# SwiGLU on one core: one activation and one product for each two-row tile in place of one for each row

**The chip and the metric.** The kernel runs on one core of one Trainium2 chip. The metric is the device time of one execution in microseconds (us). Three runs of the kernel before gave 936.18 us in the median (936.04 to 936.34).

## The reference

```python
# x: 8192 x 8192, float32, normal random numbers
def reference(x):
    a, b = np.split(x, 2, axis=-1)
    silu_b = b / (1 + np.exp(-b))
    return a * silu_b                 # 8192 x 4096
```

Each input row holds 4096 values `a` and then 4096 gates `b`. The kernel must read 268.44 MB and write 134.22 MB. It does two operations of arithmetic on each output: a silu and a product.

## The kernel before

A tile holds 128 partitions with two rows each, so a partition holds `a0 b0 a1 b1`, 4096 floats each: 64 KB. There are 32 tiles and three buffers. ScalarE (ACT) overwrites `b` with silu(b), and VectorE (DVE) writes the product over `a`. Row 1's product goes over `b0`, which row 0's product has read by then, so that both results lie side by side and leave in one store. SyncE (SP) issues the loads. ACT issues the stores, apart from the last three, which SP issues.

```python
    R, BUFS = 2, 3
    # ... last = 31
    def swiglu(i, k, c0=0, cw=half):
        xt = tiles[i]
        b = xt[:, k * M + half + c0 : k * M + half + c0 + cw]
        nc.scalar.activation(out=b, in_=b, func=_SILU)
        nc.vector.tensor_mul(
            out=xt[:, k * half + c0 : k * half + c0 + cw],
            in0=xt[:, k * M + c0 : k * M + c0 + cw],
            in1=b,
        )
    # ...
    for i in range(BUFS):
        load(i)
    for i in range(last):
        for k in range(R):
            swiglu(i, k)
        if i == last - 1:
            swiglu(last, 0)
        store(i)
        nxt = i + BUFS
        if nxt < last:
            load(nxt)              # waits until store(i) has landed
        elif nxt == last:
            load(last, (0, 1))     # the last tile comes in two halves
            load(last, (1, 2))
    store(last, 0, half)
    # ... the last row in two pieces, then its store
```

Of the kernel before, what the change touches and what calls it, by code (L numbers as in the profile page):

```python
# [1 line left out]

# [4 lines left out]

_SILU = mybir.ActivationFunctionType.Silu


@with_exitstack
def kernel(
    ctx: ExitStack,
    tc: tile.TileContext,
    x: bass.AP,
    out: bass.AP,
):




    nc = tc.nc
    N, M = x.shape
    half = M // 2
    P = nc.NUM_PARTITIONS
    R = 2
    BUFS = 3

    xv = x.tensor.reshape([N // R, R * M]).ap()  # L30
    ov = out.tensor.reshape([N // R, R * half]).ap()
    ntiles = N // (P * R)
    last = ntiles - 1

    pool = ctx.enter_context(tc.tile_pool(name="sbuf", bufs=BUFS))
    ctx.enter_context(tc.manual_schedule())
    tiles = {}

    def load(i, rows=None):
        if i not in tiles:  # L40
            tiles[i] = pool.tile([P, R * M], x.dtype, name="xt")
        lo, hi = (0, R) if rows is None else rows
        nc.sync.dma_start(  # L43
            out=tiles[i][:, lo * M : hi * M], in_=xv[i * P : (i + 1) * P, lo * M : hi * M]
# [9 lines that stand above are left out]
            in1=b,  # L54
        )

    def store(i, c0=0, cw=R * half):
        (nc.scalar if i < last - 1 else nc.sync).dma_start(
            out=ov[i * P : (i + 1) * P, c0 : c0 + cw], in_=tiles[i][:, c0 : c0 + cw]
        )  # L60

    for i in range(BUFS):
        load(i)
    for i in range(last):
        for k in range(R):
            swiglu(i, k)
        if i == last - 1:
            swiglu(last, 0)
        store(i)
        nxt = i + BUFS  # L70
        if nxt < last:
            load(nxt)
        elif nxt == last:
            load(last, (0, 1))
            load(last, (1, 2))

    store(last, 0, half)
    for c0 in range(0, half, half // 2):
        swiglu(last, 1, c0, half // 2)
    store(last, half, half)  # L80


# [1 line left out]
_INS = ['x']  # L84
_OUTS = [((8192, 4096), 'float32')]


# [23 lines left out]
```

## Time and profile before

| | before |
|---|---|
| span of the profiled run | 934.8 us |
| DVE / ACT busy | 30% / 25% |
| DMA rate in the steady part | 434 GB/s, share 1.00 |
| round of one buffer | 87.0 us: load 34.4, compute 12.6, store 39.7 |
| period of a tile | 29.0 us |

What a load or a store takes beyond the 29.0 us of a tile is waiting behind another one in its queue: 5.4 us for the load and 10.6 for the store that the prediction follows. "Queueing" below means this waiting, and "room" means the queueing of a load and a store together; the prediction works both out.

### The profile page before, as it was taken

Reading aid. Unit: us, or ns where it says so; the run is one execution under the profiler, and the core shown is the slowest. Engines: PE = TensorE matmul, PEld = TensorE weight load, DVE = VectorE, ACT = ScalarE, POOL = GpSimd, SP = SyncE. Lnnn points to the kernel's source line nnn. Section 1 sums busy time; section 2 is a strip of 40 time slices with the busy share of each in tenths; the row PEclk is TensorE's granted clock in tenths of the full one; section 3 lists DMA queues with packets and bytes.
Section 4 is the critical chain, followed back from the end, with each engine's and each line's share of the span. In section 5 each row is a group of like instructions: output and inputs, shape, how many; then the busy total and the mean of one; then the engine's idle time right before and its main releaser. Section 6 shows DMA issues by size and latency. Waiting matters only on the chain.

```text
span 934.8 us, 367 instructions
## 1 busy us (share of the span) xinstructions
DVE 283.3 (30%) x65; ACT 229.4 (25%) x66; POOL 0.2 (0%) x4
## 2 busy tenths in 40 slices
DVE  0333312333123331133321333213332133331242
ACT  0223320233302333113331133311333203332041
POOL 0000000000000000000000000000000000000000
DMA  9999999999999999999999999999999999999998
GB/s 404 400 445 430 430 439 433 428 435 443 428 430 439 429 442 432 435 426 453 419 430 452 411 452 423 428 447 425 433 433 453 414 443 429 426 447 428 425 437 376
DMA packets 9506, 402.67 MB, mean 431 GB/s; under 512 B 1056, under 2 KB 1056, under 8 KB 1056
## 3 DMA queue, kind: packets, MB, share of 16 engines
q1 hardware_dynamic: 5184, 276.83, 68.6%
q10 hardware_dynamic: 4320, 125.83, 31.2%
q14 instruction: 2, 0.02, 0.0%
HBM read 268.44 MB, written 134.22 MB: 431 GB/s over the span
## 4 chain that ended last, share of the span: by engine, by line
DMA 84%; DVE 10%; ACT 4%; DVEq 0%; issue 0%; SPq 0%; ACTq 0%
DMA out_dram<-xt 42%; DMA xt<-in_x_dram 42%; DVE xt L51 10%; ACT xt L50 4%; DVEq L106 0%; SPq L43 0%; ACTq L50 0%; DVEq L51 0%
## 5 line engine op out<-in xcount | busy, mean ns | idle before, releaser
L51 DVE TENSOR_TENSOR xt<-xt 128x4096 f32<-128x4096 f32 (+1 forms) x65 | 283.3, 4359 | 637.7 <-ACT xt L50 634.5
L50 ACT ACTIVATE xt<-xt 128x4096 f32<-128x4096 f32 (+1 forms) x65 | 228.1, 3556 | 688.1 <-DMA xt<-in_x_dram 688.1
L50 ACT ACT_TABLE_LOAD x1 | 1.3, 1283 | 0.7 <-PEq L95 0.7
L95 POOL MEMSET const-bfloat16-1.0<- 128x1 bf16 x1 | 0.1, 103 | 0.0
L95 POOL MEMSET const-uint8-127<- 128x1 uint8 x1 | 0.1, 102 | 0.0
L95 POOL MEMSET const-float32-0.0<- 128x1 f32 x1 | 0.1, 100 | 0.2 <-issue 0.2
L95 POOL MEMSET const-float32-1.0<- 128x1 f32 x1 | 0.1, 99 | 0.0
## 6 DMA issues: line engine op xcount, KB each, us to landing
out_dram<-xt ACTq DMA_DIRECT2D x30, 4096.0 KB, 39.7
xt<-in_x_dram SPq DMA_DIRECT2D x2, 4096.0 KB, 27.1
out_dram<-xt SPq DMA_DIRECT2D x1, 4096.0 KB, 23.6
out_dram<-xt SPq DMA_DIRECT2D x2, 2048.0 KB, 14.5
xt<-in_x_dram SPq DMA_DIRECT2D x31, 34.5
```

The source lines that it names most:

```text
L50: nc.scalar.activation(out=b, in_=b, func=_SILU)
L51: nc.vector.tensor_mul(out=xt[:, k * half + c0 : k * half + c0 + cw], in0=xt[:, k * M + c0 : k * M + c0 + cw], in1=b,)
L95: nc = _bacc.Bacc("TRN2", target_bir_lowering=False, num_devices=1)
```

## The change

The intent is fewer and longer instructions: one activation over both gates of a tile and one product over both rows, in place of two each. The product reads `a0 a1` against `b0 b1` and writes its 8192 results to the front of the tile. The second half of its output therefore lies over `b0`, an input of the same instruction. The last tile keeps its pieces.

```diff
+    def swiglu_tile(i):
+        rows = tiles[i].rearrange("p (k s c) -> p k s c", k=R, s=2)
+        b = rows[:, :, 1, :]
+        nc.scalar.activation(out=b, in_=b, func=_SILU)
+        nc.vector.tensor_mul(
+            out=tiles[i][:, : R * half].rearrange("p (k c) -> p k c", k=R),
+            in0=rows[:, :, 0, :],
+            in1=b,
+        )
@@
     for i in range(last):
-        for k in range(R):
-            swiglu(i, k)
+        swiglu_tile(i)
```

## The prediction

Four passages that no trace of this case shows are cut from the prediction, and the cuts are marked. The first two, around the count of packets, set the rate, the sharing of the engines and the durations beside figures from elsewhere, and argued that the overlapping product would give right results at the rate of the product by rows. The third gave a reason for the small gain of rival 3, the fourth the reason for the 1% of rival 4. Rival 3's tenths and rival 4's 1% stand as guesses. No term of the sum is cut: it comes to 0 us, with 0 to 1 us for the load margin, so 936.4 against 936.18.

Two things that the prediction uses have their numbers in the packet records of the kernel before. A load's row (64 KB) took 2.418 us and a store's (32 KB) 1.213 in the median, and of those begun between 133 and 850 us 3167 were loads' and 3166 stores': 289 and 145 GB/s, two thirds and a third. And a transfer's start: load 0, issued at 0.73 us, had its first packet at 1.73. The "up to 2 us" of a restart in the range was a guess; no trace had shown a restart then, and the experiments below measured from nothing to about 1.8 us.

> **What bounds the kernel now.** I read first the page of the profile (busy shares, the span in slices), then the busy time by stage, then the chain that ended last, then the timeline of two tiles, and last the groups by shape. From the page:
>
> ```profile
> DVE 283.3 (30%) x65; ACT 229.4 (25%) x66; POOL 0.2 (0%) x4
> ...
> DMA  9999999999999999999999999999999999999998
> ...
> HBM read 268.44 MB, written 134.22 MB: 431 GB/s over the span
> ```
>
> The compute engines are busy 30% and 25% of the span; the DMA engines are at 90% or more in all slices but the last. The kernel does nothing but stream 402.67 MB through one core, so the first suspicion is that the stream sets the time. The stages say how close to its ceiling it is (columns: stretch, its length, busy time of DVE, ACT and POOL, clock, DMA share, GB/s):
>
> ```profile
> 22.00:35.00 13.00, 8.64 (x2) 7.12 (x2) 0.00 (x0) 1.00 1.00 434
> ...
> 46.00:75.00 29.00, 8.85 (x2) 7.12 (x2) 0.00 (x0) 1.00 1.00 434
> ...
> 400.00:429.00 29.00, 8.83 (x3) 7.10 (x3) 0.00 (x0) 1.00 1.00 434
> ```
>
> The share is 1.00 and the rate 434 GB/s, at 22 to 35 us (loads alone; no store is issued before 35.24 us) as in the middle (loads and stores together). At 434 GB/s the 402.67 MB take 927.8 us of a span of 934.8; the other 7 us are mostly start and end (nothing moves in the first microsecond, and the last 2.8 us move at 29 GB/s). So in the steady part there is almost no idle time of the DMA that a change of the computing could win back.
>
> The page's chain of work seems to object: it gives 84% to DMA, 10% to DVE and 4% to ACT, as though 14% were computing on the path. The chain in order of time shows one round of a buffer (columns: start, length, what; in us):
>
> ```profile
> 98.96 34.44 DMA xt<-in_x_dram
> ...
> 133.51 3.63 ACT xt L50
> ...
> 137.16 4.43 DVE xt L51
> ...
> 141.68 4.44 DVE xt L51
> ...
> 146.14 39.70 DMA out_dram<-xt
> ```
>
> A buffer goes round in load 34.44, compute 12.6 (133.51 to 146.12), store 39.70, and a few tenths of issue: 87.0 us. There are three buffers, so a tile passes every 29.0 us. Now 29.0 us is also what the bytes of one tile need: 8.39 MB in and 4.19 MB out, 12.58 MB / 434 GB/s = 29.0 us. Both descriptions give the same period, so one of them is slack. The timeline decides which (columns: start, length, engine and line, operation, count, idle time before it):
>
> ```profile
> 75.42 7.12 ACT L50 ACTIVATE xt<-xt 128x4096 f32<-128x4096 f32 x2 [21.87 <-DMA xt<-in_x_dram]
> 79.07 8.96 DVE L51 TENSOR_TENSOR xt<-xt 128x4096 f32<-128x4096 f32 x2 [20.04 <-ACT xt L50]
> 88.06 0.34 ACTq L58 DMA_DIRECT2D out_dram<-xt  x1
> 104.51 7.12 ACT L50 ACTIVATE xt<-xt 128x4096 f32<-128x4096 f32 x2 [21.96 <-DMA xt<-in_x_dram]
> 108.16 8.96 DVE L51 TENSOR_TENSOR xt<-xt 128x4096 f32<-128x4096 f32 x2 [20.13 <-ACT xt L50]
> 117.15 0.34 ACTq L58 DMA_DIRECT2D out_dram<-xt  x1
> ```
>
> The load issued at 98.96 lands at 133.40, but the load before it lands only at about 104.4 (ACT starts on it at 104.51): for 5.4 us of its 34.4 it waits behind another load. The store issued at 117.15 follows one issued at 88.06, which takes 39.7 and lands at about 127.8: it waits some 10.6 us behind a store. In the steady part there are thus always a load and a store under way, and the round carries 5.4 + 10.6 = 16.0 us of queueing. The DMA stream is the bound; compute counts on the chain only because it takes the place of queueing.
>
> [...] The page's count agrees with one packet per row: 4320 packets for 30 stores are 144 each, about 128 rows of 32 KB plus 16. A load's row is 64 KB, so a load gets about two thirds of the rate and a store a third, and both finish in about 29 us of service. [...]
>
> **The change part by part.** The durations come from the groups by shape:
>
> ```profile
> L51 DVE TENSOR_TENSOR xt<-xt 128x4096 f32<-128x4096 f32 x63 | 278.8, 4425 | 634.2 <-ACT xt L50 631.0
> L50 ACT ACTIVATE xt<-xt 128x4096 f32<-128x4096 f32 x63 | 224.4, 3608 | 682.1 <-DMA xt<-in_x_dram 682.1
> L51 DVE TENSOR_TENSOR xt<-xt 128x2048 f32<-128x2048 f32 x2 | 4.5, 2288 | 3.5 <-ACT xt L50 3.5
> L50 ACT ACTIVATE xt<-xt 128x2048 f32<-128x2048 f32 x2 | 3.7, 1901 | 6.0 <-DMA xt<-in_x_dram 6.0
> ```
>
> Slopes and fixed parts: DVE (4425-2288)/2048 = 1.043 ns an element and 151 ns fixed; ACT (3608-1901)/2048 = 0.833 and 194. The whole-tile forms have 8192 elements: DVE 151 + 8192 x 1.043 = 8.70 us, ACT 194 + 8192 x 0.833 = 7.02 us.
> - Removed on 31 tiles (tile 31 keeps its pieces): one ACTIVATE and one product each, so 62 instructions, and their fixed parts. DVE saves 2 x 4.425 - 8.70 = 0.15 us a tile, 4.7 us in all; ACT saves little, since neighbours overlap already (two take 7.12, one is to take 7.02), 0.1 a tile. Neither is on the path that sets the end: both engines idle about 20 us before each tile.
> - Moved: the first product used to begin after the first ACTIVATE, 3.63 us after the tile landed, beside the second. Now it waits for the whole 7.02. From landing to the issue of the store: before 88.06 - 75.42 = 12.64 us; after 7.02 + 8.70 + about 0.08 of gaps = 15.80. That is 3.16 us more per tile, 98 us over 31 tiles if it were all exposed.
> - Unchanged: bytes, packets, issuing queues, number and size of transfers.
>
> What becomes of the 3.16 us: the round was 16.0 us of queueing, 58 of service (29 each way) and 13 of compute and issue. With 3.16 more of compute the queueing falls to about 12.8, and no store or load can leave the DMA without work: while one queue has a transfer pending the engines stay at 434. Predicted for the steady part: 29.0 us a tile as before.
>
> The start: no store can go before tile 0 is done, so store 0 is issued at about 38.4 instead of 35.24. For those 3.16 us only loads run, but at 434 too, and nothing is lost. It moves the phase: store 0 was issued at 35.24, landed at about 69.9 (the first wait of SP's queue at the load line ends there), 5.5 us before load 2 landed at 75.4. Store 0 would now land near 73.1, while load 2, with 3.16 us of sole use (0.46 MB ahead, worth 1.6 us at two thirds of the rate), lands near 73.8. So the margin in the load queue falls from 5.5 to about 0.7 us, less than a transfer's start, and the load queue may run dry for a microsecond at a tile boundary. Then the stores, which are queued by 10 us, take the whole rate, land sooner and let the next load go sooner: the balance mends itself.
>
> The end: tile 30 lands at 887.99 and its store is issued at 900.62; after the change near 904. That store goes out on the same queue as the two half loads of tile 31, behind them, and these land only at 904.9 and 914.5. So the later issue is hidden. After 914.5 three stores (8.39 MB) are left, 19.3 us at 434; the last of them is issued at 921.0, while the others still have some 8 us to go. Tile 31's pieces are untouched, and DVE is free for them (tile 30's product ends near 904, the first piece starts at 908.6). Sum: 0 us, with perhaps 0 to 1 us for the thinner load margin. I predict 936.4 against 936.18.
>
> **Rivals.**
> 1. *The later store is exposed.* The chain's 14% of computing is real, and each round grows by 3.16 us: a third of that per tile with three buffers, 1.05 x 31 = 33 us, to about 969. For it: the chain as printed. Against: 16 us of queueing in each round, and DMA share 1.00. I give it 2%.
> 2. *The load queue runs dry and the rate falls.* If each tile lost half a microsecond to a restart that the stores do not fill, it would cost 31 x 0.5 = 15 us, to about 951; with 0.1 us, 3 us. For it: the margin that shrinks to about 0.7 us, and the stores-only stretch at the end runs at 410 to 421 GB/s. Against: loads alone keep 434, and stores are queued. A small part of this is what widens my range upwards.
> 3. *Fewer instructions make it faster.* The 4.7 us of DVE time saved would show only if DVE bound; it idles two thirds of the time. At most the total shrinks by some tenths[...]. It would give about 935.5.
> 4. *The strided or overlapping form is slow,* say at half rate: DVE 17 us, ACT 14, 31 us a tile. Then the compute, one after the other, would eat the queueing, and the kernel would go to perhaps 980. [...] 1%.
>
> **Range and chances.** The three runs of before lie within 0.3 us, so noise is small. The range comes from the restart effect (up to 2 us) and the phase of the ends (1 us either way): 935.2 to 938.6. A 2% step is 18.7 us, which needs rival 1 or 4, or rival 2 at more than half a microsecond a tile. Chances: faster 0.01, same 0.96, slower 0.03.
>
> **What would show it.** Right: whole-tile products near 8.70 us and activations near 7.02; 15.8 us from a tile's landing to its store; DMA share still 1.00 and 434 GB/s; landings of tiles still 29.0 us apart; times from issue to landing of loads and stores together some 3.2 us shorter (74.2 to about 71); in the chain the computing grows from 14% to 18% and DMA falls to about 80%, with the span unchanged. Wrong: a landing period above 29.1 us, a stage with less than 430 GB/s in the middle, or products much longer than 8.7 us.

## More of the kernel before

All runs reported here are with a granted clock of 1.00.

The prediction shows most of the lines. Three more are needed later. The first is the page's chain of work that ended last, by engine. The second and third are from its list of transfers (queue that issues, count, KB each, median us from issue to landing; the list gives no size for the last, the 31 loads of a whole tile).

```profile
DMA 84%; DVE 10%; ACT 4%; DVEq 0%; issue 0%; SPq 0%; ACTq 0%
...
out_dram<-xt ACTq DMA_DIRECT2D x30, 4096.0 KB, 39.7
...
xt<-in_x_dram SPq DMA_DIRECT2D x31, 34.5
```

## The result

The changed kernel took 937.08 us in the median of four runs (936.9 to 937.74), and the kernel before took 936.26 in four (936.04 to 936.64). The ratio is 1.001, with a 95% interval of 0.9992 to 1.0027: the same within 2%. The four runs of each do not overlap, but the interval includes 1, so this pair alone does not show the 0.8 us between the medians to be real. A ratio here is the mean time of one kernel's fast runs over that of the other's in the same rounds, so it is not quite the ratio of the medians quoted. The results are correct.

The page of the changed kernel has these lines for the engines, the bytes, the chain and the transfers:

```profile
DVE 278.4 (30%) x34; ACT 226.5 (24%) x35; POOL 0.2 (0%) x4
...
HBM read 268.44 MB, written 134.22 MB: 430 GB/s over the span
...
DMA 81%; DVE 10%; ACT 8%; DVEq 0%; issue 0%; SPq 0%; ACTq 0%
...
out_dram<-xt ACTq DMA_DIRECT2D x30, 4096.0 KB, 34.9
...
xt<-in_x_dram SPq DMA_DIRECT2D x31, 36.2
```

DVE's busy time fell by 4.9 us, and the total did not follow. Computing on the chain rose from 14% to 17% (13.8% and 17.2% before the page rounds its parts), some 3.1 us for each tile that the chain passes, and the DMA part of the chain fell by as much, because transfers wait less. A load and a store together took 34.5 + 39.7 = 74.2 us before and 36.2 + 34.9 = 71.1 now. That is the 3.1 us. The groups by shape give the new instructions (count, then busy us and mean ns, then idle time before them and what ended it):

```profile
L62 DVE TENSOR_TENSOR xt<-xt 128x8192 f32<-128x8192 f32 x31 | 269.4, 8692 | 635.5 <-ACT xt L61 635.5
L61 ACT ACTIVATE xt<-xt 128x8192 f32<-128x8192 f32 x31 | 217.9, 7029 | 676.3 <-DMA xt<-in_x_dram 676.3
```

The timeline of the changed kernel shows two steady tiles:

```profile
802.16 7.03 ACT L61 ACTIVATE xt<-xt 128x8192 f32<-128x8192 f32 x1 [21.98 <-DMA xt<-in_x_dram]
809.22 8.69 DVE L62 TENSOR_TENSOR xt<-xt 128x8192 f32<-128x8192 f32 x1 [20.32 <-ACT xt L61]
817.94 0.34 ACTq L69 DMA_DIRECT2D out_dram<-xt  x1
...
831.16 7.03 ACT L61 ACTIVATE xt<-xt 128x8192 f32<-128x8192 f32 x1 [21.97 <-DMA xt<-in_x_dram]
```

From a tile's landing to its store is now 817.94 - 802.16 = 15.78 us, where it was 12.64, and yet the next tile lands after the same 29.00 us.

The small loss of the profiled run (span 936.0 against 934.8) is at the start. Busy time by stage of the changed kernel (stretch, length, DVE, ACT and POOL busy, clock, DMA share, GB/s):

```profile
46.00:75.00 29.00, 8.69 (x1) 5.76 (x2) 0.00 (x0) 1.00 0.97 421
75.00:104.00 29.00, 8.69 (x1) 4.34 (x1) 0.00 (x0) 1.00 1.01 419
104.00:133.00 29.00, 8.69 (x1) 7.03 (x1) 0.00 (x0) 1.00 0.99 429
133.00:162.00 29.00, 8.69 (x1) 7.03 (x1) 0.00 (x0) 1.00 1.00 434
```

Before, the first two of these stages had 434 and 433 GB/s. The three shortfalls from 434 are (13 + 15 + 5) x 29 / 434 = 2.2 us. Some 0.7 of that is given back, because the stage just ahead (35 to 46 us) went from 366 to 393 GB/s, 27 x 11 / 434. From 133 us on the rate is 434, as before. SP's queue and the timeline of the changed kernel tell what happened at that boundary; here is the issue of load 3:

```profile
72.56 0.33 SPq L43 DMA_DIRECT2D xt<-in_x_dram  x1
```

The two activations that wait for load 2 and for load 3 start here:

```profile
72.31 7.03 ACT L61 ACTIVATE xt<-xt 128x8192 f32<-128x8192 f32 x1 [23.23 <-DMA xt<-in_x_dram]
...
108.57 7.03 ACT L61 ACTIVATE xt<-xt 128x8192 f32<-128x8192 f32 x1 [29.23 <-DMA xt<-in_x_dram]
```

Load 2 had landed just before 72.31, and load 3 could only be issued at 72.56, when store 0 had landed. The load queue was empty, and by the packet records of the trace no load packet was under way from 71.9 to 77.4 us. Before, load 3 was issued at 69.94 and load 2 landed at about 75.4. So tile 3 is ready at 108.57 where it was ready at 104.51. After two more tiles the landings are 29.0 us apart again, with 1.2 us of delay left at the end.

### The profile page after: what moved, and what is told of

Read it like the earlier page. It is cut to its first block, busy times and chain, and to the rows that moved or that the text cites. A ratio compares the mean times of both kernels' runs of the same rounds, so it can differ in the third digit from the quotient of the medians.

```text
span 936.0 us, 302 instructions
## 1 busy us (share of the span) xinstructions
DVE 278.4 (30%) x34; ACT 226.5 (24%) x35; POOL 0.2 (0%) x4
## 4 chain that ended last, share of the span: by engine, by line
DMA 81%; DVE 10%; ACT 8%; DVEq 0%; issue 0%; SPq 0%; ACTq 0%
DMA xt<-in_x_dram 43%; DMA out_dram<-xt 37%; DVE xt L62 9%; ACT xt L61 8%; DVE xt L51 0%; DVEq L116 0%; ACT xt L50 0%; SPq L43 0%; ACTq L61 0%
## 5 line engine op out<-in xcount | busy, mean ns | idle before, releaser
L62 DVE TENSOR_TENSOR xt<-xt 128x8192 f32<-128x8192 f32 x31 | 269.4, 8692 | 635.5 <-ACT xt L61 635.5
L61 ACT ACTIVATE xt<-xt 128x8192 f32<-128x8192 f32 x31 | 217.9, 7029 | 676.3 <-DMA xt<-in_x_dram 676.3
L51 DVE TENSOR_TENSOR xt<-xt 128x2048 f32<-128x2048 f32 (+1 forms) x3 | 8.9, 3000 | 8.3 <-ACT xt L50 8.3
L50 ACT ACTIVATE xt<-xt 128x2048 f32<-128x2048 f32 (+1 forms) x3 | 7.3, 2473 | 15.9 <-DMA xt<-in_x_dram 15.9
## 6 DMA issues: line engine op xcount, KB each, us to landing
out_dram<-xt ACTq DMA_DIRECT2D x30, 4096.0 KB, 34.9
xt<-in_x_dram SPq DMA_DIRECT2D x31, 36.2
```

The source lines that it names most:

```text
L51: nc.vector.tensor_mul(out=xt[:, k * half + c0 : k * half + c0 + cw], in0=xt[:, k * M + c0 : k * M + c0 + cw], in1=b,)
L62: nc.vector.tensor_mul(out=tiles[i][:, : R * half].rearrange("p (k c) -> p k c", k=R), in0=rows[:, :, 0, :], in1=b,)
```

## The experiments

Two questions were tested. First, is the additional 3.1 us of each tile a real latency that is hidden (theory), and not one that the chain of work would charge to the total, shared by three buffers (rival)? Second, where do the 0.8 us come from, once at the start or a little in each tile? All eleven kernels gave correct results.

### One buffer: is the latency real?

Both kernels with no room to hide anything (the row by row one is shown; the other has the same edit):

```diff
-    BUFS = 3
+    BUFS = 1
@@
-        if i == last - 1:
-            swiglu(last, 0)
@@
+    swiglu(last, 0)
     store(last, 0, half)
```

By rows:

> The kernel before with one buffer in place of three: load, compute and store of a tile follow one another. Both theories: load alone 21.4 us (tile 0's load in the profile of before took that), compute 12.6, store alone about 11.9, some tenths of issue: 46.6 us a tile, in all about 1480 to 1500 us. It is the base for the next run.

By tiles:

> The changed kernel with one buffer. Here nothing can hide the compute, so both theories expect the whole extra time from landing to store, 3.13 us x 31 tiles = 97 us more than the one-buffer kernel by rows, about 1580 to 1595 us. If the difference were well under 97, the extra 3.13 us would not be a real latency, and the result with three buffers would need no hiding at all.

By rows it took 1456.26 us (1456.07 to 1456.51), by tiles 1552.93 (1552.59 to 1553.35). The difference is 96.7 us, against an expected 97: the latency is real, and adds 6.6% to the kernel in which nothing lies beside it. The absolute times came out some 25 us under the lower ends of my estimates. The chain of the one-buffer kernel by tiles (start, length, what) shows why:

```profile
429.20 11.10 DMA out_dram<-xt
...
440.37 21.82 DMA xt<-in_x_dram
...
462.28 7.04 ACT xt L61
...
469.34 8.70 DVE xt L62
```

The tile's store takes 11.10 us alone and not 11.9, and the gaps between the pieces come to 0.2 us and not the 0.7 that my sum of 46.6 left for them; the load is 0.4 us longer than I put it. Load and store together are 32.9 us where the bytes need 29.0, so two lone transfers cost about 3.9 us of starts and ends. (By transfer, 21.82 - 19.3 = 2.5 us for the load and 11.10 - 9.7 = 1.4 for the store; the next expectation puts about 2 us for each.)

### Two buffers: does less room bring the latency out?

```diff
-    BUFS = 3
+    BUFS = 2
```

By rows:

> The kernel before with two buffers: the base for the next run. A buffer's store and the load after it follow one another with a start between them (about 2 us each), and while the other buffer is being computed nothing fills that gap: some 2 us a tile over the 29.0 that the bytes need, about 985 to 1010 us.

By tiles:

> The changed kernel with two buffers. My theory: the DMA engines lose time only when no transfer at all is pending; while one buffer is computed for 15.8 us the other one transfers for over 29, so the longer compute is hidden here too, all but the starts: 0 to 10 us more than by rows. Rival (computing on the chain counts in full and is shared by the buffers): 3.13 / 2 x 31 = 49 us more than by rows.

By rows it took 1052.38 us (1051.16 to 1054.13), by tiles 1046.32 (1043.92 to 1046.8). The rival's 49 us are refuted: the longer compute cost nothing, and the kernel by tiles was even 6 us faster, which neither side expected. My base was wrong too: 116 us over the three-buffer kernel, and not 50 to 75. One stage of each shows the state of the stream, first by rows:

```profile
499.00:532.00 33.00, 8.85 (x2) 7.12 (x2) 0.00 (x0) 1.00 0.93 384
```

Then by tiles:

```profile
499.00:532.00 33.00, 8.69 (x1) 7.03 (x1) 0.00 (x0) 1.00 0.94 385
```

These are typical: four adjoining stages have 382 GB/s by rows and 384 by tiles in the mean. The engines idle for only some 6% of the time, but the rate is 12% below 434. By the times of issue and landing, no transfer at all was pending for only 1.8 us in either kernel, so my theory of when time is lost is wrong here too. In the packet records of the trace a load's packet (one row, 64 KB) takes 2.418 us when the stream is steady. I summed, per DMA engine, the time by which packets of loads ran over that: 54.6 us in the two-buffer kernel by rows and 46.1 by tiles, against 2.2 in the kernel before. The time without any packet (span less packet time, per engine) was 62.4 and 65.7, against 2.1. So these kernels lose time in two ways: idle engines and slow packets. The two profiled runs differ by 4.7 us: by tiles, slow load packets took 8.5 us less, and the engines idled 3.3 us more. Why slow packets cost less by tiles, I did not settle.

### Tile 0 alone: once, or in each tile?

The changed kernel with tile 0 back to rows:

```diff
-        swiglu_tile(i)
+        if i > 0:
+            swiglu_tile(i)
+        for k in range(R if i == 0 else 0):
+            swiglu(i, k)
```

> The changed kernel, but tile 0 computed by rows as before, so that store 0 goes out at 35.2 and not 38.4 us. Theory (the 0.8 us that the changed kernel lost come once, at the first boundary, where the load queue ran dry): load 3 lands near 104.5 again instead of 108.5, and the time is 936.0 to 936.6, as before. Rival (a restart lost at each tile, or whole-tile instructions slower for the stream): 937.0, as the changed kernel.

The kernel before with tile 0 alone as a whole (the reverse edit):

> The kernel before, with tile 0 alone computed as a whole. Theory (lost once at the start): all of the 0.8 us, 936.8 to 937.4, with load 3 landing near 108. Rival (lost per tile): 1/31 of it, 936.2 to 936.3.

On one chip in the same rounds: changed kernel with tile 0 by rows 935.78 us (935.69 to 936.21), kernel before 936.33 (935.88 to 936.88), kernel before with tile 0 alone as a whole 937.00 (936.84 to 937.38). The first lies 0.2 us under the range that my theory gave, the last inside its own. The first and the last do not overlap, and are 1.2 us apart; neither alone is shown to differ from the kernel before. Load 3 was ready at 104.62 us in the first (its activation starts there) and at 107.90 in the last, as my theory has it. The stage from 75 us on tells the same, first with tile 0 alone by rows:

```profile
75.00:104.00 29.00, 8.69 (x1) 7.03 (x1) 0.00 (x0) 1.00 1.00 434
```

Then with tile 0 alone as a whole:

```profile
75.00:104.00 29.00, 8.85 (x2) 4.13 (x2) 0.00 (x0) 1.00 1.02 420
```

The loss follows tile 0. Thirty whole tiles cost nothing that these runs can see; the one first tile costs all of it. The ratios to the kernel before are 0.9995 (interval 0.9983 to 1.0008) and 1.0008 (0.9996 to 1.0021).

### More compute in every tile: where does the room end?

The changed kernel with one, two or four copies of the result onto itself after each product:

```diff
         swiglu_tile(i)
+        for _ in range(2):            # 1, 2 or 4
+            p = tiles[i][:, : R * half]
+            nc.vector.tensor_copy(out=p, in_=p)
```

Two copies, submitted first together with four:

> The changed kernel with two copies of the result onto itself on DVE before each store, about 4.4 us each: from landing to store some 24.6 us instead of 15.8. Theory: 24.6 is still under the 29.0 that a tile's bytes need, so a transfer is always pending: within 4 us of the changed kernel, queueing in the round down from about 13 to about 4 us. Rival (the chain counts): 8.8 / 3 x 31 = 91 us more, about 1028.

Four copies:

> Four copies: about 33.4 us from landing to store. Over 29.0, so the compute becomes the bound: ACT's queue issues the store of a tile before it starts on the next tile, so tiles pass every 33.7 to 33.9 us: 22.6 + 31 x 33.8 + about 23 for the end, 1080 to 1110 us, DMA share well under 1.00. Rival (the chain counts): 17.6 / 3 x 31 = 182 us more, about 1119. The two copies and the four together show where the slack ends; if four are also within 10 us, the theory of where it ends is wrong.

One copy:

> The changed kernel with one copy on DVE, 4.43 us, before each store: 20.2 us from landing to store. Two copies cost 26 us more than the changed kernel, against my theory (at most 4) and against the chain (91). New theory: engines have work as long as one queue does, but a queue that ran dry pays about 1 us to start again, and how often it does so depends on the queueing left in the round; here 29.0 - 20.2 = 8.8 us are left, against 13 in the changed kernel (one restart, at the start) and 4.4 with two copies (nearly one for each tile). So few restarts: 1 to 6 us more than the changed kernel, 938 to 943. A loss in proportion to the added time would be half of 26: 950. The chain: 46 more, 983.

| copies | start of the activation to store, us | time, us (lowest to highest) |
|---|---|---|
| 0 (the changed kernel) | 15.8 | 937.08 (936.9 to 937.74) |
| 1 | 20.3 | 937.31 (935.96 to 938.68) |
| 2 | 24.8 | 962.74 (960.26 to 969.0) |
| 4 | 33.7 | 1104.69 (1104.63 to 1104.86) |

No run before these had timed a copy; the 62 of the two-copy kernel took 4.427 us each in the mean. The "about 1 us" of a restart in the new theory compares with the 1.2 us between the two tile 0 kernels. One copy fits the new theory and is not shown to be slower than the changed kernel; its four runs fall into two pairs, near 936.0 and near 938.6, and only one of the faster pair was profiled. Up to two copies the activation starts as the tile lands in the steady part, so the second column is also the time from landing to store there; with four it waits for DVE. Four copies came out as my sum had it: compute is the bound, and its timeline has the activation of the next tile waiting for DVE and no longer for a load.

```profile
432.07 7.03 ACT L61 ACTIVATE xt<-xt 128x8192 f32<-128x8192 f32 x1 [27.09 <-DVE xt L79]
...
466.20 7.03 ACT L61 ACTIVATE xt<-xt 128x8192 f32<-128x8192 f32 x1 [27.10 <-DVE xt L79]
```

The period there is 466.20 - 432.07 = 34.13 us, a little over the 33.7 to 33.9 expected. The rival's sum (1119) is only 14 us off here; it is the wait for DVE that shows the bound. Two copies refuted both sides: 26 us more than the changed kernel, where my theory allowed 4 and the rival asked for 91. Its stages:

```profile
400.00:429.00 29.00, 14.27 (x4) 7.03 (x1) 0.00 (x0) 1.00 1.00 434
429.00:458.00 29.00, 18.91 (x4) 7.03 (x1) 0.00 (x0) 1.00 0.98 397
500.00:529.00 29.00, 17.55 (x3) 5.31 (x2) 0.00 (x0) 1.00 0.99 430
```

The share stays near 1, but the rate drops now and then. In its packet records, by my count, loads had no packet under way 13 times (for over 1.5 us) and stores 9 times (for over 3 us) between the start and the last tile; in the one-copy kernel's profiled run that was once each, and in the kernel before never. The sums of above, against the kernel before: slow load packets +16.4 us, slow store packets +6.0, engines without a packet +8.7. Together that is 31.1 of the 32.4 us by which this profiled run (the slowest of its four, 969.0) has the longer span. The slow packets come in clusters beside such gaps, though not every gap has one. By the times of issue and landing, no transfer at all was pending for only 0.1 us of this run. So it does not suffice that some transfer is pending. Both queues should stay non-empty, and at 29.0 - 24.8 = 4.2 us of queueing in the round they do not.

### One disturbance in the middle: what does a restart cost?

The kernel before with copies on tile 15 alone:

```diff
         for k in range(R):
             swiglu(i, k)
+        for _ in range(2 if i == 15 else 0):     # 2 or 4
+            p = tiles[i][:, : R * half]
+            nc.vector.tensor_copy(out=p, in_=p)
```

Two copies:

> The kernel before, with two copies (8.86 us) added on tile 15 alone, in the middle of the stream. Its store waits 10.6 us behind another store anyhow, so it lands as before: no difference, within 0.3 us of the kernel before, and the landings of loads stay 29.0 apart. The chain, shared by three buffers: 3.0 us more.

Four copies:

> The kernel before, with four copies (17.7 us) on tile 15 alone. That is over the 10.6 us for which the store waits in its queue: the store queue runs dry for some 7 us while loads have the engines, the store lands later, and the load queue then runs dry once. The engines keep work all along. New theory: one or two restarts, 0.7 to 2 us more than the kernel before. If the engines keep their rate whatever the queues do: under 0.3. The chain: 5.9 us more.

On one chip: two copies 936.08 us (935.59 to 936.93), kernel before 936.38 (935.4 to 938.11), four copies 937.55 (937.12 to 938.28). With two copies the stage of tile 15 runs at full rate:

```profile
458.00:487.00 29.00, 17.83 (x5) 7.25 (x3) 0.00 (x0) 1.00 1.00 433
```

With four, that stage and the one after it do not, and the next one does again:

```profile
458.00:487.00 29.00, 24.69 (x6) 5.18 (x3) 0.00 (x0) 1.00 1.04 430
487.00:516.00 29.00, 14.64 (x4) 10.67 (x4) 0.00 (x0) 1.00 0.96 415
516.00:545.00 29.00, 3.06 (x1) 2.10 (x1) 0.00 (x0) 1.00 1.00 434
```

So 8.9 us of delay cost nothing that can be seen, and 17.8 us cost 1.2 in the medians. The runs with two copies and with four do not overlap, but those of the kernel before cover both, and the intervals of the two ratios (0.9985 to 1.001 and 0.9999 to 1.0026) overlap. The chain would have said 3.0 and 5.9. In the packet records of the second kernel the store queue had nothing pending for 6.5 us, from landing to issue (I expected some 7), and was without a packet for 12.6; some 17 us after that the load queue was without one for 8.0. Of the slow load packets, 1.3 us in all, 0.5 came just after the stores had run out and 0.8 just before they began again, and almost none came with the restart of the loads. In the one-copy kernel's profiled run (935.96 us, the fastest of its four) the load queue was without a packet for 6.7 us at the start, and no packet was slow after it. In the two-copy kernel the slow packets beside one such gap come to as much as 1.8 us. So running dry costs from nothing to about 1.8 us in slow packets, and what decides that stays open.

## Why the prediction was right

**The bound.** It held. The middle of the changed kernel runs at 434 GB/s and a tile passes every 29.00 us. Of the stages of 29 us that were read, only the three between 46 and 133 us are under 430 GB/s, which in the middle would have been the prediction's sign of being wrong.

**The size of the parts.** Predicted were 8.70 and 7.02 us for the new instructions and 15.80 from landing to store; the trace has 8.692, 7.029 and 15.78. The overlapping product gave correct results and was no slower by element than the product by rows: (8692 - 4425) / 4096 = 1.042 ns for each further element, against the slope of 1.043 from 2048 to 4096. DVE's saving was 4.9 us against 4.7. That one-buffer kernels differ by 96.7 us shows that the latency is real.

**What becomes of it.** Queueing in the round was to fall from 16.0 to 12.8. It fell to 7.2 for loads (36.2 - 29.0) plus 5.9 for stores, 13.1. Restoring or adding latency in single tiles and in all of them shows that this is the mechanism: 4.4 us more per tile (one copy) were hidden as well, and 8.9 more (two copies) were not.

**The start.** The step was right in kind: store 0 went out at 38.39 and the load queue ran dry once. It was mis-sized in two places. Store 0 landed at 72.5 (predicted 73.1), and load 2 landed at 72.3 (predicted 73.8), so the margin was not +0.7 but about -0.2. Load 2 came earlier because store 0's packets began only at 44.5 us, 6.1 after its issue, by the packet records; before they began at 39.5, 4.2 after it. So loads ran alone for 5.0 us more, not 3.16; worked as in the prediction, that is 2.5 us of the 3.1 by which load 2 came earlier. With no other load or store under way, load 0's packets had begun 1.0 us after its issue (0.73 to 1.73). The second place is that the load queue was to run dry "for a microsecond": it was without a packet for 5.5 us (71.9 to 77.4), 4.9 of them after load 3 had been issued. That the balance mends itself came true: in the steady part it is 7.2 for loads and 5.9 for stores.

**"The stores take the whole rate."** This step was too good. The stores filled all 16 engines while no load packet was under way (71.9 to 77.4 us: share 1.00, 413 GB/s by the packet records), but the restart itself was slow: load packets begun between 58 and 87 us took 0.9 us an engine too long, and store packets 0.3. Less the 0.4 us that slow packets cost less where store 0 sets in, and with 0.3 us more of idle engines, this is the 1.2 us between the two profiled spans. The medians differ by 0.8 us, inside the 0 to 1 us that the sum allowed; that it stayed so small was partly luck, as the same gap cost nothing in the one-copy run and such gaps cost up to 1.8 us with two copies.

**The end.** Store 30 was issued at 904.93 (predicted 904) and cost nothing; by the packet records its rows began only at about 913, behind those of the half loads. From the landing of the last load to the end are 20.3 us in both kernels (934.8 - 914.5 and 936.0 - 915.7).

**The rivals.** Rival 1 (the chain counts) was refuted in every test but two: in the one-buffer pair the chain has no queueing in it, and with four copies the two sums lie too close. Rival 2 (the load queue runs dry and the rate falls) is real: once in the changed kernel, and over much of the stream when 24.8 us of compute leave 4.2 us of room. Rival 3's gain did not come. Rival 4 is refuted by the durations, 8.69 and 7.03 us where it had 17 and 14. What the prediction argued, that the engines stay at 434 "while one queue has a transfer pending", is the part that the two-copy kernel disproved: a transfer was pending for all but 0.1 us of it, and it lost 26 us. The changed kernel, with 13.1 us of queueing left, was far enough from that edge for it to matter only at the start.

## What to carry to other kernels

In a kernel bound by transfers, read how much of a transfer's time from issue to landing is queueing (here time to landing minus the period): compute latency could grow by less than this here before anything was seen. Of the 13.1 us in the changed kernel, 4.4 could be taken at no cost that these runs show, and taking 8.9 cost 26 us. The chain of work that ended last does not tell it, since it charges the queueing's place to whatever filled it: its computing went from 13.8% to 17.2%, and a tile still passed every 29.0 us. Keep some microseconds of queueing for loads and for stores separately (7.2 and 5.9 kept 434 GB/s here; 4.2 for both together did not), above all at the start, where the first store decides when the first reused buffer is loaded; merging instructions lengthened the way to the store from 12.64 to 15.78 us, so leave the first tile fine-grained, or accept about a microsecond (0.8 us in the medians here).
